# Two edits in the MLP of a hybrid encoder: a later row of norm factors, and a last step by plain products

## The chip, the cores and the metric

The kernel runs on one core of a Trainium2 chip, in one launch. The metric is the device time of that launch in microseconds; the median of three runs is 1983.71 us (1982.65 to 1984.13). The engines are named as in the profile: PE (TensorE's matrix products), PEld (its weight loads), DVE (VectorE), ACT (ScalarE), POOL (GpSimd), SP (SyncE, which here issues nearly all transfers).

## The reference, cut to what matters

x is 256 positions by 2048 channels, in float32. Two mixer layers, each followed by the MLP that this case is about:

```
def rmsnorm(x, g):
    y = xf * lax.rsqrt(jnp.mean(xf * xf, axis=-1, keepdims=True) + EPS)
    return y * g
def sq_relu_mlp(h, w_up, w_down):          # w_up 2048 x 8192, w_down 8192 x 2048
    a = jnp.square(jax.nn.relu(jnp.einsum('bsd,df->bsf', h, w_up)))
    return jnp.einsum('bsf,fd->bsd', a, w_down)
for i in range(2):
    ...
    x = x + sq_relu_mlp(rmsnorm(x, mlp_norm[i]), w_up[i], w_down[i])
return rmsnorm(x, final_norm)
```

## The kernel before, in words

**Products.** Every float32 operand is split into a high part (fp32r) and the rest. `split_piece` (L71) does so for 1024 columns of weights: ACT casts (`whi`, L73), DVE subtracts (`wlo`, L74); each side has four buffers. A block product is three matmuls into one PSUM bank (`mm3`, L105 to L108). `linear` (L110) computes one group of 512 output columns for both halves of the positions (t = 0, 1) in two banks of the pool `accp` (four banks), over 16 tiles of 128 inputs, and calls hooks before some of these tiles.

**Start of an MLP.** Before it, the last `linear` of the mixer's output projection ends, `add_x` adds its banks to x (L228, one add per t), `stats` squares x on ACT (L207), DVE and POOL turn the sums into the norm factor r per position (L213 to L218). r is needed along the free dimension, so L632 to L640 build a row of it: DVE scales the identity (`dg`, L634), PE multiplies ones by that (`rb`, L637, two float32 matmuls, which the trace shows as four), ACT copies the bank to `rb` (L639). r itself enters only later, in `hidden` (L687). The up products use x transposed and scaled by the norm's gain alone (`act`); the last quarter of it is made by `chunk(3)` (eight PE transposes, L197, then four copies on ACT, L187, and four on DVE, L188), a hook ahead of the fourth tile of the first up piece.

**Up.** One unit u makes 128 hidden channels for all positions: 16 weight tiles in two pieces (p = 0, 1), eight wide matmuls with the high weights (`high`, L659) and eight half as wide with the low ones (`low`, L651) for each. Units 0 and 1 open an MLP, their pieces interleaved: (unit 0, p 0), (unit 1, p 0), (unit 0, p 1), (unit 1, p 1). `hidden(q, z)` takes the two units of step q: times r, relu, square, split, and four block sums for the step below.

**Down.** Step q multiplies 256 hidden channels into 1024 of the 2048 output columns. As two by two blocks that is done by seven block products in place of eight: 21 matmuls, into the banks Q1, P2, Q3, Q5 (`accp`) and Q7, Q6, Q4 (the pool `tpp`, also four banks). Weights come by `s_load` (L709) and, summed, by `s_sums` (L720). Eight steps make a cycle, four cycles an MLP. In the code step c of cycle g issues unit 2q, the first three products of step q - 1, unit 2q + 1, and the other four; `more` is false in the very last step, which has no units left. After a cycle `s_end` (L738) adds the seven banks into x, and two `linear` calls do the other 1024 columns (n = 2, 3) for the cycle's 16 hidden tiles, with plain products. In the last cycle `stats` and `chunk` of the next norm follow: (0), (1) after `s_end`, (2) after n = 2, (3) after n = 3. In the second MLP `nxt` is `Final` (L576): its `stats` squares on ACT and multiplies by the gain on DVE (L589), its `chunk` does nothing, and n = 3 runs with three open banks and the kernel's end behind it.

**Order.** The text of the program is a list; a scheduler of the framework reorders it and fixes one order for each engine. On the chip every engine takes its list strictly in that order.

Of the kernel before, what the change touches and what calls it, by code (L numbers as in the profile page):

```python
# [12 lines left out]
F32 = mybir.dt.float32  # L13
# [6 lines left out]
P = 128  # L20
S = 256
# [7 lines left out]
PIECE = 2048  # L29
HALF = 1024  # L30
# [13 lines left out]
def trunk_kernel(ctx, tc, x_in, x_t, small, w_in_e0, w_in_e, w_out_e, w_in_o, w_lat2, w_uqn, w_uqr, w_ukv, w_out_o,  # L44
                 w_up0, w_up1, w_ds0, w_ds1, w_dn0, w_dn1, g_fin, dft_s, dft_c, rope, out):
    nc = tc.nc
# [9 lines left out]
    accp = ctx.enter_context(tc.tile_pool(name="accp", bufs=4, space=PSUM))  # L56
    tpp = ctx.enter_context(tc.tile_pool(name="tpp", bufs=4, space=PSUM))
# [5 lines left out]
    ones = const.tile([P, P], F32, name="ones")  # L63

    def load_raw(dram, n):
        raw = rawp.tile([P, PIECE], F32, tag="raw", name="raw")
        nc.sync.dma_start(out=raw[:, :n], in_=dram)
        return raw

    def split_piece(raw, o, n):  # L70
        hi = whp.tile([P, HALF], F32R, tag="whi", name="whi")  # L71
        lo = wlp.tile([P, HALF], F32R, tag="wlo", name="wlo")
        nc.scalar.copy(out=hi[:, :n], in_=raw[:, o:o + n])  # L73
        nc.vector.tensor_tensor(out=lo[:, :n], in0=raw[:, o:o + n], in1=hi[:, :n].bitcast(F32), op=ALU.subtract)  # L74
        return hi, lo
# [91 lines left out]
    def mm_kt(acc, t, a, part, j, n, first, last, c0=0, c1=None):  # L167
        sl = slice(t * P, (t + 1) * P)
        hi, lo = part
        c1 = c1 or n  # L170
        ws = slice(j * n + c0, j * n + c1)
        mm3(acc[t][:, c0:c1], a[0][:, sl], a[1][:, sl], hi[:, ws], lo[:, ws], first, last)
# [51 lines left out]
    def add_x(acc, n, scale=None, ts=(0, 1)):  # L224
        for t in ts:
            sl = xs[:, t, n * 512:(n + 1) * 512]
            if scale is None:
                nc.vector.tensor_tensor(out=sl, in0=acc[t], in1=sl, op=ALU.add)  # L228
            else:
                nc.vector.scalar_tensor_tensor(out=sl, in0=acc[t], scalar=scale[:, t:t + 1], in1=sl,  # L230
                                               op0=ALU.mult, op1=ALU.add)
# [388 lines left out]
    def mlp(ni, pend, w_up, w_ds, w_dn, nxt):  # L620
# [4 lines left out]
        G, C = 4, 8  # L625
# [6 lines left out]
        dg = stg.tile([P, 2, P], F32, tag="stg", name="dg", bufs=4)  # L632
        for t in range(2):
            nc.vector.tensor_scalar(out=dg[:, t, :], in0=ident, scalar1=ni.r[:, t:t + 1], scalar2=None, op0=ALU.mult)  # L634
        tp = tpp.tile([P, S], F32, tag="tp", name="rb")
        for t in range(2):
            nc.tensor.matmul(out=tp[:, t * P:(t + 1) * P], lhsT=ones, rhs=dg[:, t, :], start=True, stop=True)  # L637
        rb = mp_.tile([P, S], F32, name="rb")
        nc.scalar.copy(out=rb, in_=tp)  # L639
        rb2 = rb.rearrange("p (o c) -> p o c", o=1).broadcast_to([P, 2, S])  # L640

        def up_open(u):
            return u, tpp.tile([P, 512], F32, tag="tp", name="accT"), load_raw(w_up[u], PIECE)

        def up_piece(o, p, hooks):
            u, acc, raw = o
            hi, lo = split_piece(raw, p * HALF, HALF)

            def low():
                for k in range(8):  # L650
                    nc.tensor.matmul(out=acc[:, S:], lhsT=lo[:, k * P:(k + 1) * P], rhs=act[8 * p + k][0],  # L651
                                     start=False, stop=False)

            def high():
                for k in range(8):
                    kt = 8 * p + k
                    for f in hooks.get(kt, ()):
                        f()
                    nc.tensor.matmul(out=acc, lhsT=hi[:, k * P:(k + 1) * P], rhs=act[kt][2],  # L659
                                     start=kt == 0, stop=kt == 15)  # L660
            if p == 0:
                high()
                low()
            else:
                low()
                high()

        def up_end(o, z):
            u, acc, _ = o
            j = u % 2  # L670
            nc.scalar.copy(out=z[:, j, :], in_=acc[:, S:])  # L671
            nc.vector.tensor_tensor(out=z[:, j, :], in0=acc[:, :S], in1=z[:, j, :], op=ALU.add)  # L672

        def new_z():
            return stg.tile([P, 2, S], F32, tag="stg", name="z", bufs=4)
# [6 lines left out]
        def hidden(q, z):  # L682

            if q % 2 == 0:
                pool, tag = (mp_, "hx") if q // 2 % 5 == 4 else (a8p, "a8")
                slots[q // 2] = pool.tile([P, 2, 2, 512], F32R, tag=tag, name="hT")
            nc.vector.scalar_tensor_tensor(out=z, in0=z, scalar=0.0, in1=rb2, op0=ALU.max, op1=ALU.mult)  # L687
            h = stg.tile([P, 4, P], F32, tag="stg", name="h", bufs=4)
            nc.scalar.activation(out=h.rearrange("p a b -> p (a b)"), in_=z.rearrange("p a b -> p (a b)"),
                                 func=AF.Square)  # L690
            a = pair(q)
            split_from(h.rearrange("p a b -> p (a b)"), a[:, 0, :], a[:, 1, :])
            x = stg.tile([P, 4, P], F32, tag="stg", name="x", bufs=4)
            nc.vector.tensor_tensor(out=x[:, 0:2, :], in0=h[:, 0:2, :], in1=h[:, 2::-2, :], op=ALU.subtract)
            nc.vector.tensor_tensor(out=x[:, 2, :], in0=h[:, 1, :], in1=x[:, 0, :], op=ALU.subtract)
            nc.vector.tensor_tensor(out=x[:, 3, :], in0=h[:, 3, :], in1=x[:, 2, :], op=ALU.subtract)
            xh = mp_.tile([P, 4, P], F32R, tag="xh", name="xh")
            xl = mp_.tile([P, 4, P], F32R, tag="xl", name="xl")
            split_from(x, xh, xl)
            xs_of[q] = xh, xl  # L700
# [37 lines left out]
        def s_end(b):  # L738
# [11 lines left out]
            add(xc(0, 0), xc(0, 0), u)  # L750
            add(xc(0, 1), xc(0, 1), u, ALU.subtract)


        z = new_z()
        os = [up_open(u) for u in range(2)]
        for p in range(2):
            for j in range(2):
                up_piece(os[j], p, pend if j == p == 0 else {})
        for o in os:
            up_end(o, z)  # L760
        hidden(0, z)
        pend = {}
        for g in range(G):
            last = g == G - 1
            b = {}
            for c in range(1, C + 1):
                q = g * C + c
                f, l = c == 1, c == C
                more = q < G * C
                if more:  # L770
                    z = new_z()
                    o = up_open(2 * q)
                    for p in range(2):
                        up_piece(o, p, {})
                    up_end(o, z)
                r4, bh, bl = s_load(q - 1)
                if f:
                    b = {n: accp.tile([P, 512], F32, tag="acc", name=n) for n in ("Q1", "P2", "Q3", "Q5")}
                prod(b["Q1"], block(q - 1, 1), bh, bl, 0, f, l)
                prod(b["P2"], block(q - 1, 3), bh, bl, 2, f, l)  # L780
                prod(b["Q3"], xsum(q - 1, 3), bh, bl, 1, f, l)
                th, tl = s_sums(r4)
                if more:
                    o = up_open(2 * q + 1)
                    for p in range(2):
                        up_piece(o, p, {})
                    up_end(o, z)
                if f:
                    b.update({n: tpp.tile([P, 512], F32, tag="tp", name=n) for n in ("Q7", "Q6", "Q4")})
                prod(b["Q5"], xsum(q - 1, 0), th, tl, 1, f, l)  # L790
                prod(b["Q7"], xsum(q - 1, 1), th, tl, 0, f, l)
                if more:
                    hidden(q, z)
                prod(b["Q6"], xsum(q - 1, 2), th, tl, 2, f, l)
                prod(b["Q4"], block(q - 1, 2), th, tl, 3, f, l)
            s_end(b)
            if last:
                nxt.stats(0)
                nxt.stats(1)
                pend = {3: [lambda: nxt.chunk(0)], 7: [lambda: nxt.chunk(1)]}  # L800
            hT = [tuple(pair(g * C + k // 2)[:, i, (k % 2) * S:(k % 2 + 1) * S] for i in range(2)) for k in range(2 * C)]
            for n in (2, 3):
                if last and n == 3 and isinstance(nxt, Final):
                    linear(hT, list(range(16)), w_dn[2 * g + n - 2], 0, 512, halves=True, done=nxt.last, early=8)
                    st.close()
                    return {}
                acc = linear(hT, list(range(16)), w_dn[2 * g + n - 2], 0, 512, hooks=pend)
                pend = {}
                add_x(acc, n)
                if last:  # L810
                    nxt.stats(n)
                    pend = {3: [lambda n=n: nxt.chunk(n)]}
        st.close()
        return pend

# [405 lines left out]
```

## Time and profile before

| What | Value |
| --- | --- |
| median of the runs | 1983.71 us (1982.65 to 1984.13) |
| profiled execution, own time | 1980.53 us |
| its span, first to last instruction | 1978.7 us |
| PE busy, instructions | 1947.4 us (98%), 9868 |
| DVE, ACT busy | 1574.8 us (80%), 1133.6 us (57%) |
| mean granted TensorE clock | 0.997 |

A matmul's row shows from when to when it was in the array; the next one starts before it ends, so what a matmul costs is read from start to start. A bracket at a row's end is idle time of the engine just before, and what ended it. Busy time at a lower clock is busy time too: it takes the rows of granted clock to see it.

### The profile page before, as it was taken

The page shows a single profiled execution, that of the slowest core. Times are in us where ns is not written, and L with a number is a line of the kernel's source. Part 1 is how long each engine was busy: PE and PEld are TensorE (multiplying, and loading weights), DVE is VectorE, ACT ScalarE, POOL GpSimd, SP SyncE. Part 2 cuts the span into 40 slices and gives each one's busy share as a digit, 9 for nine tenths or more (in the row PEclk, how much of TensorE's full clock was granted, in tenths as well). Part 3 has the DMA queues.
Part 4 walks back from the last instruction along what each step waited for, and adds up shares of the span by engine and source line. Part 5 has one row for each costly group of instructions (what it writes and reads, how often), then busy time and mean ns, then how long its engine had stood idle before and what let it go on. Part 6 is the DMA issues. An engine that isn't in the chain of part 4 may idle for free.

```text
span 1978.7 us, 25204 instructions
## 1 busy us (share of the span) xinstructions
PE 1947.4 (98%) x9868; PEld 1650.1 (83%) x9868; DVE 1574.8 (80%) x2195; ACT 1133.6 (57%) x1583; POOL 11.6 (1%) x19
## 2 busy tenths in 40 slices
PE   8999999999999999999999999999999999999998
PEld 7887778888888888887888888788888888888877
DVE  7999768878896887887576667588968878896895
ACT  6787655645654664565554545456546645654654
POOL 0000000000000000000000000000000000000000
PEclk9999999999999999999999999999999999999999
DMA  8554545555555555454454546455555555555542
GB/s 296 200 174 167 210 155 175 204 199 189 192 192 213 192 195 206 174 198 148 160 189 149 190 169 241 165 192 191 181 209 190 204 198 189 192 191 213 192 170 107
DMA packets 55207, 374.00 MB, mean 189 GB/s; under 512 B 6064, under 2 KB 6448, under 8 KB 11824
## 3 DMA queue, kind: packets, MB, share of 16 engines
q1 hardware_dynamic: 54656, 370.69, 53.3%
q8 instruction: 77, 1.26, 0.3%
q0 software_dynamic: 144, 1.05, 0.1%
q10 hardware_dynamic: 288, 0.66, 0.1%
q14 instruction: 42, 0.34, 0.1%
HBM read 370.27 MB, written 2.10 MB: 188 GB/s over the span
## 4 chain that ended last, share of the span: by engine, by line
PE 93%; DVE 3%; DMA 1%; ACT 1%; issue 1%; POOL 0%; SPq 0%; POOLq 0%; DVEq 0%; ACTq 0%
PE accT L659 23%; PE acc L107 13%; PE acc L106 13%; PE acc L108 13%; PE accT L651 12%; PE Q L108 4%; PE Q L106 4%; PE Q L107 4%; PE tp L106 1%; PE tp L107 1%; PE tp L108 1%; DVE wlo L74 1%; PE P L107 1%; PE P L106 1%; PE P L108 1%
## 5 line engine op out<-in xcount | busy, mean ns | idle before, releaser
L74 DVE TENSOR_TENSOR wlo<-raw,whi 128x1024 fp32r<-128x1024 f32 (+2 forms) x568 | 683.4, 1211 | 312.5 <-ACT whi L73 311.9
L73 ACT CAST whi<-raw 128x1024 fp32r<-128x1024 f32 (+2 forms) x568 | 592.2, 1044 | 466.7 <-PE acc L108 307.9
L659 PE MATMUL accT<-n,whi 128*128 128x512 f32 x2048 | 514.5, 393 | 0.1
L659 PEld LDWEIGHTS accT<-n,whi 128*128 128x128 f32 x2048 | 377.3, 189 | 75.9 <-DVE z L672 0.6
L651 PEld LDWEIGHTS accT<-n,wlo 128*128 128x128 f32 x2048 | 262.9, 191 | 10.2
L651 PE MATMUL accT<-n,wlo 128*128 128x256 f32 x2048 | 266.0, 283 | 0.0
L107 PE MATMUL acc<-wlo,hT 128*128 128x512 f32 (+1 forms) x528 | 203.3, 385 | 0.1
L108 PE MATMUL acc<-whi,hT 128*128 128x512 f32 (+1 forms) x528 | 202.8, 384 | 0.0
L106 PE MATMUL acc<-whi,hT 128*128 128x512 f32 (+1 forms) x528 | 202.0, 384 | 0.0
L106 PE MATMUL acc<-whi,n 128*128 128x512 f32 (+2 forms) x480 | 181.1, 379 | 7.1 <-ACT whi L73 7.0
L107 PE MATMUL acc<-wlo,n 128*128 128x512 f32 (+2 forms) x480 | 178.4, 372 | 0.8 <-DVE wlo L74 0.8
L108 PE MATMUL acc<-whi,n 128*128 128x512 f32 (+2 forms) x480 | 178.7, 373 | 0.0
L722 DVE TENSOR_TENSOR sraw<-sraw 128x512 f32<-128x512 f32 x256 | 174.8, 683 | 1.0
L185 DVE TENSOR_TENSOR tl<-sraw,th 128x1024 fp32r<-128x1024 f32 x128 | 155.6, 1216 | 0.3
L184 ACT CAST th<-sraw 128x1024 fp32r<-128x1024 f32 x128 | 132.6, 1043 | 6.5 <-DVE sraw L722 3.5
L671 ACT COPY z<-accT 128x256 f32<-128x256 f32 x128 | 47.9, 375 | 150.7 <-PE accT L659 150.7
L185 DVE TENSOR_TENSOR bl<-sraw,bh 128x512 fp32r<-128x512 f32 (+1 forms) x128 | 118.5, 952 | 17.7 <-ACT bh L184 17.4
L184 ACT CAST bh<-sraw 128x512 fp32r<-128x512 f32 (+1 forms) x128 | 100.7, 834 | 30.5 <-DMA sraw<-in_w_ds 24.5
L107 PEld LDWEIGHTS acc<-wlo,hT 128*128 128x128 f32 x528 | 99.2, 188 | 22.0 <-DVE wlo L74 2.4
L106 PEld LDWEIGHTS acc<-whi,hT 128*128 128x128 f32 x528 | 99.2, 188 | 20.6 <-DVE xs L736 0.4
L108 PEld LDWEIGHTS acc<-whi,hT 128*128 128x128 f32 x528 | 99.2, 188 | 19.8
L106 PEld LDWEIGHTS acc<-whi,n 128*128 128x128 f32 x480 | 90.9, 190 | 21.2 <-ACT whi L73 7.8
(287 smaller groups left out, 2550.5 us busy)
## 6 DMA issues: line engine op xcount, KB each, us to landing
raw<-in_w_up SPq DMA_DIRECT2D x128, 1024.0 KB, 4.8
sraw<-in_w_ds SPq DMA_DIRECT2D x64, 1024.0 KB, 4.8
raw<-in_w_dn SPq DMA_DIRECT2D x64, 1024.0 KB, 4.9
raw<-in_w_in_o SPq DMA_DIRECT2D x28, 1024.0 KB, 4.9
raw<-in_w_in_e SPq DMA_DIRECT2D x20, 1024.0 KB, 5.0
raw<-in_w_out_e SPq DMA_DIRECT2D x16, 1024.0 KB, 5.0
raw<-in_w_out_o SPq DMA_DIRECT2D x16, 1024.0 KB, 4.8
raw<-in_w_in_e SPq DMA_DIRECT2D x6, 512.0 KB, 4.4
```

The costliest lines, as they stand in the source:

```text
L73: nc.scalar.copy(out=hi[:, :n], in_=raw[:, o:o + n])
L74: nc.vector.tensor_tensor(out=lo[:, :n], in0=raw[:, o:o + n], in1=hi[:, :n].bitcast(F32), op=ALU.subtract)
L106: nc.tensor.matmul(out=outs, lhsT=hi, rhs=rhi, start=first, stop=False)
L107: nc.tensor.matmul(out=outs, lhsT=hi, rhs=rlo, start=False, stop=False)
L108: nc.tensor.matmul(out=outs, lhsT=lo, rhs=rhi, start=False, stop=last)
L184: nc.scalar.copy(out=hi, in_=src)
L185: nc.vector.tensor_tensor(out=lo, in0=src, in1=hi.bitcast(F32), op=ALU.subtract)
L651: nc.tensor.matmul(out=acc[:, S:], lhsT=lo[:, k * P:(k + 1) * P], rhs=act[8 * p + k][0], start=False, stop=False)
L659: nc.tensor.matmul(out=acc, lhsT=hi[:, k * P:(k + 1) * P], rhs=act[kt][2], start=kt == 0, stop=kt == 15)
L671: nc.scalar.copy(out=z[:, j, :], in_=acc[:, S:])
L722: nc.vector.tensor_tensor(out=r4[:, o, :], in0=r4[:, i0, :], in1=r4[:, i1, :], op=ALU.add)
```

## The change

Two edits, both in `mlp`, which runs twice.

1. The two matmuls of the norm row and ACT's copy of it become a function, `rstd_row`, called after the p 0 pieces of units 0 and 1. The identity's scaling on DVE (`dg`) stays where it was.
2. In the last cycle the loop runs seven steps, not eight. The eighth step (hidden channels of step 31) is done by `rest`, after `linear` of n = 2: its weights come through the common weight buffers, unsummed, and its eight block products (24 matmuls) go into two pairs of `accp` banks, each pair added to x by `add_x`. So x's columns of n = 0, 1 are final only then: `stats` (0), (1), (2) come after `rest`, and their `chunk`s are hooks of n = 3. `more` goes, as every step left in the loop has units.

```
-        tp = tpp.tile([P, S], F32, tag="tp", name="rb")
-        for t in range(2):
-            nc.tensor.matmul(out=tp[:, t * P:(t + 1) * P], lhsT=ones, rhs=dg[:, t, :], start=True, stop=True)
         rb = mp_.tile([P, S], F32, name="rb")
-        nc.scalar.copy(out=rb, in_=tp)
...
+        def rstd_row():
+            tp = tpp.tile([P, S], F32, tag="tp", name="rb")
+            for t in range(2):
+                nc.tensor.matmul(out=tp[:, t * P:(t + 1) * P], lhsT=ones, rhs=dg[:, t, :], start=True, stop=True)
+            nc.scalar.copy(out=rb, in_=tp)
...
+        def rest(hT):
+            raw = load_raw(w_ds[G * C - 1], PIECE)
+            parts = [split_piece(raw, o, HALF) for o in (0, HALF)]
+            for n in range(2):
+                acc = [accp.tile([P, 512], F32, tag="acc", name=f"acc{t}") for t in range(2)]
+                for k in range(2):
+                    for t in range(2):
+                        mm_kt(acc, t, hT[2 * C - 2 + k], parts[k], 1 - n, 512, k == 0, k == 1)
+                add_x(acc, n)
...
                 up_piece(os[j], p, pend if j == p == 0 else {})
+            if p == 0:
+                rstd_row()
...
-            for c in range(1, C + 1):
+            steps = C - 1 if last else C
+            for c in range(1, steps + 1):
...
             s_end(b)
-            if last:
-                nxt.stats(0)
-                nxt.stats(1)
-                pend = {3: [lambda: nxt.chunk(0)], 7: [lambda: nxt.chunk(1)]}
...
-                if last:
-                    nxt.stats(n)
-                    pend = {3: [lambda n=n: nxt.chunk(n)]}
+                if last and n == 2:
+                    rest(hT)
+                    for m in (0, 1, 2):
+                        nxt.stats(m)
+                        pend[4 * m + 3] = [lambda m=m: nxt.chunk(m)]
+                elif last:
+                    nxt.stats(3)
+                    pend = {3: [lambda: nxt.chunk(3)]}
```

How the order on the engines moves, at three places. First PE at the start of the first MLP, before: acc1 is the last bank of the projection, accT_2299 and accT_2302 are units 0 and 1, n10 to n13 the transposed x in four parts, tp the banks of the transposes.

```order
L108 MATMUL acc1_2187<-whi_2258,ya1_1868 128x512
L637 MATMUL rb_2293<-dg_2290,ones_86 128x128 x2
L659 MATMUL accT_2299<-n10_1921,whi_2305 128x512 x3
L197 MATMUL tp_2312<-ident_84,xs_82 128x128 x4
L197 MATMUL tp_2321<-ident_84,xs_82 128x128 x4
L659 MATMUL accT_2299<-n10_1921,whi_2305 128x512
L659 MATMUL accT_2299<-n11_1922,whi_2305 128x512 x4
L651 MATMUL accT_2299<-n10_1921,wlo_2306 128x256 x4
L651 MATMUL accT_2299<-n11_1922,wlo_2306 128x256 x4
```

The same place on PE after the change, from the transposes on; the row ahead of them is the first three matmuls of unit 0 (accT_2295), and ahead of these stands the last of acc1.

```order
L197 MATMUL tp_2308<-ident_84,xs_82 128x128
L197 MATMUL tp_2317<-ident_84,xs_82 128x128
L661 MATMUL accT_2295<-n10_1921,whi_2301 128x512
L197 MATMUL tp_2308<-ident_84,xs_82 128x128 x3
L197 MATMUL tp_2317<-ident_84,xs_82 128x128 x3
L661 MATMUL accT_2295<-n11_1922,whi_2301 128x512 x4
L653 MATMUL accT_2295<-n10_1921,wlo_2302 128x256 x4
L653 MATMUL accT_2295<-n11_1922,wlo_2302 128x256 x4
L661 MATMUL accT_2298<-n10_1921,whi_2339 128x512 x4
L661 MATMUL accT_2298<-n11_1922,whi_2339 128x512 x4
L653 MATMUL accT_2298<-n10_1921,wlo_2340 128x256 x4
L653 MATMUL accT_2298<-n11_1922,wlo_2340 128x256 x4
L641 MATMUL rb_2359<-dg_2290,ones_86 128x128 x2
```

The row's matmuls moved behind 32 up matmuls and the eight transposes, and the first two transposes (one of each bank, both of t = 0) moved ahead of the fourth up matmul. Second, PE at the end of the first MLP's last cycle, before: the last product of the seventh step, the first rows of the eighth, and its end with the start of n = 2 (acc0).

```order
L108 MATMUL Q4_6892<-th_7703,hT_7616 128x512
L106 MATMUL Q1_6822<-bh_7781,hT_7616 128x512
L107 MATMUL Q1_6822<-bl_7782,hT_7616 128x512
...
L108 MATMUL Q6_6891<-th_7800,xl_7770 128x512
L107 MATMUL Q4_6892<-tl_7801,hT_7616 128x512
L108 MATMUL Q4_6892<-th_7800,hT_7616 128x512
L106 MATMUL acc0_7840<-whi_7844,hT_6454 128x512
```

After the change, same place:

```order
L108 MATMUL Q6_6891<-th_7703,xl_7627 128x512
L106 MATMUL Q4_6892<-th_7703,hT_7616 128x512
L107 MATMUL Q4_6892<-tl_7704,hT_7616 128x512
L108 MATMUL Q4_6892<-th_7703,hT_7616 128x512
L106 MATMUL acc0_7793<-whi_7797,hT_6454 128x512
L107 MATMUL acc0_7793<-wlo_7798,hT_6454 128x512
```

The 21 matmuls of the eighth step are gone from between the seventh step and n = 2; 24 stand behind n = 2. Third, ACT after the change, from the end of the first MLP's last cycle to its last chunk copies: casts of n = 2, `rest` and n = 3 (L73), squares of `stats` (L207), copies of `chunk` (L187; n_8017 to n_8019 are chunks 0 to 2).

```order
L73 CAST whi<-raw 128x1024 x7
L207 ACTIVATE junk,n2s<-xs 128x512 x2
L73 CAST whi<-raw 128x1024 x2
L207 ACTIVATE junk,n2s<-xs 128x512 x3
L73 CAST whi<-raw 128x1024
L207 ACTIVATE junk,n2s<-xs 128x512
L187 ACTIVATE n_8017<-tp,sm 128x256 x3
L73 CAST whi<-raw 128x1024
L187 ACTIVATE n_8017<-tp,sm 128x256
L73 CAST whi<-raw 128x1024
L187 ACTIVATE n_8018<-tp,sm 128x256 x4
L73 CAST whi<-raw 128x1024 x2
```

Six squares and twelve chunk copies now stand between the casts of n = 3. Before, four squares and eight copies stood between those of n = 2, and two squares and four copies between those of n = 3.

## Rows read from the trace of the kernel before

**Rows 1.** The page: span, and busy time of each engine.
```profile
span 1978.7 us, 25204 instructions
...
PE 1947.4 (98%) x9868; PEld 1650.1 (83%) x9868; DVE 1574.8 (80%) x2195; ACT 1133.6 (57%) x1583; POOL 11.6 (1%) x19
```

**Rows 2.** Waits of PE: who waited for whom, total us, times, longest.
```profile
PE rb L637 <- DVE dg L634: 8.2, 2, 4.1
...
PE Q L106 <- ACT hT L184: 3.7, 2, 1.9
```

**Rows 3.** Timeline of PE, first MLP's start: start us, length us, instruction, idle before.
```profile
253.17 0.39 PE L108 MATMUL acc<-whi,ya 128*128 128x512 f32 x1
257.65 1.19 PE L637 MATMUL rb<-dg,ones 128*128 128x128 f32 x4 [4.09 <-DVE dg L634]
...
263.27 1.11 PE L651 MATMUL accT<-n,wlo 128*128 128x256 f32 x8
264.22 2.00 PE L659 MATMUL accT<-n,whi 128*128 128x512 f32 x8
266.06 2.08 PE L651 MATMUL accT<-n,wlo 128*128 128x256 f32 x16
```

**Rows 4.** Timeline of PE, second MLP's start.
```profile
1270.69 0.39 PE L108 MATMUL acc<-whi,yc 128*128 128x512 f32 x1
1275.21 0.68 PE L637 MATMUL rb<-dg,ones 128*128 128x128 f32 x4 [4.13 <-DVE dg L634]
1275.65 0.96 PE L659 MATMUL accT<-n,whi 128*128 128x512 f32 x3
...
1282.86 2.08 PE L651 MATMUL accT<-n,wlo 128*128 128x256 f32 x16
```

**Rows 5.** Windows: length, busy PE, PEld, DVE, ACT, POOL; clock, DMA share, GB/s.
```profile
256.00:257.00 1.00, 0.00 (x0) 0.00 (x0) 0.33 (x2) 0.01 (x1) 0.51 (x1) 0.50 0.98 418
...
1277.00:1278.00 1.00, 1.00 (x8) 1.00 (x6) 0.00 (x0) 0.47 (x1) 0.00 (x0) 0.50 0.55 221
...
906.00:908.00 2.00, 0.79 (x4) 0.30 (x3) 2.00 (x3) 1.41 (x3) 0.00 (x0) 1.00 0.90 381
```

**Rows 6.** Timeline of DVE and ACT, first MLP's start.
```profile
253.10 1.28 DVE L228 TENSOR_TENSOR xs<-acc,xs 128x512 f32<-128x512 f32 x2
...
254.54 0.63 ACT L207 ACTIVATE junk<-xs 128x512 bf16<-128x512 f32 x1
...
257.21 0.48 DVE L634 TENSOR_SCALAR dg<-ident,n1r 128x128 f32<-128x128 f32 x2 [0.80 <-POOL n1r L218]
...
261.01 0.47 ACT L187 ACTIVATE n<-tp,sm 128x256 fp32r<-128x256 f32 x1 [1.76 <-PE tp L197]
...
261.52 0.48 DVE L188 SCALAR_TENSOR_TENSOR n<-tp,sm,n 128x256 fp32r<-128x256 f32 x1 [3.82 <-ACT n L187]
```

**Rows 7.** Timeline of PE, last cycles of the first and second MLP.
```profile
902.35 0.40 PE L108 MATMUL Q<-th,hT 128*128 128x512 f32 x1
...
911.31 0.39 PE L106 MATMUL acc<-whi,hT 128*128 128x512 f32 x1
...
1917.35 0.40 PE L108 MATMUL Q<-th,hT 128*128 128x512 f32 x1
...
1926.33 0.39 PE L106 MATMUL acc<-whi,hT 128*128 128x512 f32 x1
```

**Rows 8.** Timeline of PE: n = 2 after the third cycle; chunk(0) in the last.
```profile
746.57 0.39 PE L106 MATMUL acc<-whi,hT 128*128 128x512 f32 x1
...
915.88 1.03 PE L197 MATMUL tp<-ident,xs 128*128 128x128 f32 x8
916.67 0.48 PE L108 MATMUL acc<-whi,hT 128*128 128x512 f32 x1
```

**Rows 9.** The page's groups: busy us, mean ns | idle before, what ended most.
```profile
L74 DVE TENSOR_TENSOR wlo<-raw,whi 128x1024 fp32r<-128x1024 f32 (+2 forms) x568 | 683.4, 1211 | 312.5 <-ACT whi L73 311.9
L73 ACT CAST whi<-raw 128x1024 fp32r<-128x1024 f32 (+2 forms) x568 | 592.2, 1044 | 466.7 <-PE acc L108 307.9
```

More of the change, by code (lines that the diff above doesn't have):

```diff
@@ L765, in mlp @@
             b = {}
-            for c in range(1, C + 1):
+            steps = C - 1 if last else C
+            for c in range(1, steps + 1):
                 q = g * C + c
[L768 to L775, printed above, removed]
+                f, l = c == 1, c == steps
+                z = new_z()
+                o = up_open(2 * q)
+                for p in range(2):
+                    up_piece(o, p, {})
+                up_end(o, z)
                 r4, bh, bl = s_load(q - 1)
@@ L782, in mlp @@
                 th, tl = s_sums(r4)
[L783 to L787, printed above, removed]
+                o = up_open(2 * q + 1)
+                for p in range(2):
+                    up_piece(o, p, {})
+                up_end(o, z)
                 if f:
@@ L791, in mlp @@
                 prod(b["Q7"], xsum(q - 1, 1), th, tl, 0, f, l)
-                if more:
-                    hidden(q, z)
+                hidden(q, z)
                 prod(b["Q6"], xsum(q - 1, 2), th, tl, 2, f, l)
@@ L807, in mlp @@
                 acc = linear(hT, list(range(16)), w_dn[2 * g + n - 2], 0, 512, hooks=pend)
-                pend = {}
                 add_x(acc, n)
-                if last:
-                    nxt.stats(n)
-                    pend = {3: [lambda n=n: nxt.chunk(n)]}
+                if last and n == 2:
[6 more added lines that the diff above has]
+                    pend = {3: [lambda: nxt.chunk(3)]}
         st.close()
```

## The prediction

> **What bounds the kernel now.** I read the page first: PE is busy 1947.4 of 1978.7 us [rows 1], so all that PE is free to lose is 31.3 us, and a change is worth what it takes from PE's own line: idle time, a lower clock, or matmuls. Second, PE's waits: the norm row (`rb`) waits for `dg` twice, 8.2 us in all, and the first product of the last cycles' eighth step waits for `hidden`'s cast twice, 3.7 us [rows 2]. The reader is to see that both sit exactly where the two edits are. Third, PE's timeline at these four places [rows 3, 4, 7], read from start to start: the busy share hides that the stretch behind an idle time can be slow. Fourth, the granted clock: at the starts of both MLPs it is 0.50 of full speed, the 1.2 GHz level, a while after PE stopped, with products running at that level in the second; it is 1.00, 2.4 GHz, within the eighth step though PE was idle for half of that window [rows 5].
>
> Rates at full clock: a wide up matmul (266.06 - 264.22) / 8 = 0.23; eight lows 264.22 - 263.27 = 0.95 [rows 3]; the row's four matmuls 1275.65 - 1275.21 = 0.44 [rows 4]; eight transposes 916.67 - 915.88 = 0.79 [rows 8]. I take 0.23 for every wide matmul.
>
> **Edit 1, the start of an MLP.** Nothing is removed or added; two matmuls and a copy move behind 32 up matmuls and eight transposes. Before, the projection's last matmul starts at 253.17, so PE is free for the next at 253.40. The row of 16 lows at 266.06 is (unit 1, p 0) and then (unit 0, p 1); its second half starts at 266.06 + 0.95 = 267.01 [rows 3]. By then PE has done all that in the new order stands ahead of the same point: 3 wide (0.69), eight transposes (0.79), 5 wide (1.15), eight lows (0.95), eight wide (1.84), eight lows (0.95), 6.37 in all, and the row (0.44): 6.81. Without a wait the new order gets there at 253.40 + 6.81 = 260.21: 6.80 us earlier. In the second MLP PE is free at 1270.92, so 1277.73 against 1282.86 + 0.95 = 1283.81: 6.08 earlier [rows 4]. Sum 12.88. Of it 8.2 is the wait [rows 2], and the rest, 4.7, is nearly all the half clock behind it.
>
> Does a wait take its place? The first two transposes need only the add of t = 0, and PE reaches them at 253.40 + 0.69 = 254.09; the other six need both adds, which end at 253.10 + 1.28 = 254.38 [rows 6], and PE reaches them after two transposes and a matmul, at 254.09 + 0.20 + 0.23 = 254.52. That is even; I take no wait, and 0.3 a layer as the other end. The up matmuls' weights are no issue, since ACT is ahead of PE: most of the idle time before its casts is waiting for PE to free a buffer [rows 9]. The row now stands 6.37 behind 253.40, at 259.77. `dg` started at 257.21 [rows 6]; now one chunk copy (0.47) stands between the squares on ACT, and two of DVE's chunk instructions (0.48 each) ahead of it on DVE, so it is done by 257.21 + 0.47 + 0.96 + 0.48 = 259.12 at the latest. The row is the fifth tile on `tpp`'s four banks and needs the first transposes' bank back, but the DVE instruction that frees it stands ahead of `dg`. No wait, margin 0.65; the other end is 2 a layer, half of what it waited before [rows 2]. What reads the row (`hidden`, L687) needs both units done, over 5 us later on PE.
>
> Does the clock stay up? With no gap left the case is that of any other hand-over. The row nearest to it is the eighth step: PE busy 0.79 of 2.00 us and the clock still 1.00 [rows 5]. So I take full clock, and half clock as the other end: before, PE took 266.06 - 257.65 = 8.41 and 1282.86 - 1275.21 = 7.65 from the row to the group of 16, where full rates give 6.81 - 0.95 = 5.86; the lower clock cost at most 2.55 + 1.79 = 4.3. The Trainium skill (TensorE: Matmul & The Clock Gate, part 4 on PE-mode transpose) says that transposes do not count as busy time for the clock in the way matmuls do. By that rule eight transposes right at the hand-over would be time in which the clock can fall, and the sum would be smaller by what a fall costs. This trace has chunk(0)'s transposes amid matmuls at full rate [rows 8], which is no sign of it.
>
> **Edit 2, the last cycle.** Before, from the slot behind the seventh step to the first matmul of n = 2: 911.31 - 902.35 - 0.23 = 8.73 us, and 1926.33 - 1917.35 - 0.23 = 8.75 in the second MLP [rows 7]. All of that leaves this place: 21 matmuls are 4.83, the rest is waiting for `hidden` of step 31, which nothing covers as there are no units left. What comes back, behind n = 2, is 24 matmuls, 24 x 0.23 = 5.52. Gain 3.21 + 3.23 = 6.44. `hidden` (31) is now needed by n = 2's fifteenth hidden tile, 14 x 6 x 0.23 = 19 us later, so its chain is covered.
>
> What is late next? n = 2 takes two banks that `s_end` must free. The third cycle ends with the same list, units ahead and all, and there n = 2 starts with no idle time before it [rows 8]: no wait; other end, all of edit 2's gain. The step's four sums and their splits leave DVE and ACT; two casts, two subtracts and four adds come. The transfers are as many as before, one of them in the common queue of weight buffers behind n = 2's: 24 matmuls per transfer as in `linear`. Then n = 3: six squares (0.63 each) and, in the first MLP, twelve copies on ACT (0.47) and twelve on DVE (0.48) [rows 6] stand between its casts. ACT then has 8 x 1.04 [rows 9] + 3.8 + 5.6 = 17.7 of n = 3's 96 x 0.23 + 3 x 0.79 = 24.5 us; DVE 8 x 1.21 + 5.8 and the adds. The third cast is the first behind squares: these need `rest`'s first adds, so 12 x 0.23 + 1.28 + 1.26 = 5.3 us after `rest` begins, its end 6.3; PE needs it at 5.52 + 2 x 2.76 = 11.0. Covered. In the second MLP n = 3 opens three banks, the third of which needs `rest`'s last pair's first add (0.64) soon after: 0 to 1 us, I take 0. Below nothing there is no room: PE has no other idle time in these places.
>
> **Sum.** 12.88 + 6.44 = 19.3 us less. Against the profiled execution's own time of 1980.53 that is 1961.2; the runs shown are 3.2 above it in the median, so 1983.7 - 19.3 = 1964.4.
>
> **The rivals.**
> - *The clock falls all the same* at both starts. For it: it fell there before, in one case after PE had stood still only from 253.56 to 256 [rows 3, 5]. Against: no such gap is left. 4.3 less: 1968.7. By the rule on transposes of the Trainium skill (TensorE: Matmul & The Clock Gate, part 4) it would go this way.
> - *The row waits at its new place.* For it: the margin of 0.65, and casts that wait for PE stand on ACT between the chunk copies. 2 a layer: 1968.4.
> - *The end gives nothing*: `s_end` or `rest` hands over late by as much as was saved. For it: four banks, all taken by Q1, P2, Q3, Q5 at the hand-over. Against: the third cycle [rows 8]. 1964.4 + 6.4 = 1970.8.
> - *Slower: n = 3 of the last cycle is bound by ACT and DVE.* The moved work lies between n = 3's casts, on strict lists; if PE drains its four buffers and then stands for all of it: first MLP 3.8 + 5.6 + 5.8, second 3.8 of squares + 6 x 0.64 of gains, and `rest`'s adds 2 x 2.56: 15.2 + 7.6 + 5.1 = 27.9, so 1992.3. It makes the kernel slower by more than can be told from 23.3 us uncovered on, most of it. Against: the 4.7 us to spare at the third cast.
>
> That the change doesn't do what it says is not one: the order shows the rows moved.
>
> **How the numbers follow.** Forecast 0.78; clock 0.06; row 0.05; end 0.06; slower rival 0.05, of which I give 0.03 to a partial form that ends within 0.2% (4 us, about what a measurement of this kernel can tell from no change) and 0.02 to the full one. The first four are all faster by over 0.2%: 0.95, 0.03, 0.02. The range reaches up to the end case, 1971; down to 1960.5, since all unknown costs but the runs' own offset to the profiled execution (their lowest is 2.1, their highest 3.6 above it) were already taken at their lower end.
>
> **What would show it.** After: PE's waits have no `rb` row and no `Q` rows for hT and xh; the clock is 1.00 through both starts; the row's matmuls start some 6.4 us after the projection's last slot; n = 2 of the last cycle starts 0.23 behind the seventh step's last product; 24 matmuls stand between n = 2 and n = 3 with no bracket behind. I am wrong if a new PE wait on a cast (L73) or on x (L228) shows in n = 3, if `rb` still has a wait, or if the clock rows at the starts still show 0.50.

## The result and the profile after

The changed kernel takes 1961.62 us in the median (1960.07 to 1964.19), the kernel before beside it 1983.92: ratio 0.9888, 95% interval 0.9875 to 0.9900, so 22.2 us less (19.8 to 24.8). Forecast were 19.3 us less and 1964.4. On another chip, beside the two halves of the change, it was 0.9891 (0.9877 to 0.9906). The profiled execution took 1960.07 us, against 1980.53 before: 20.5 less.

The page of the kernel after, as [rows 1]:

```profile
span 1958.3 us, 25215 instructions
...
PE 1942.3 (99%) x9874; PEld 1648.3 (84%) x9874; DVE 1572.0 (80%) x2191; ACT 1130.2 (58%) x1579; POOL 11.7 (1%) x19
```

PE's idle time fell from 31.3 to 16.0 us. That is 15.3 of the 20.4 us by which the span fell; the other 5.1 were busy time, in the main matmuls at half clock (the filled wait below puts these at 4.0). PE's waits after, all of them (who waited for whom, total us, times, longest), against [rows 2]:

```profile
PE acc L106 <- ACT whi L73: 6.1, 2, 5.7
PE acc L107 <- DVE wlo L74: 0.8, 1, 0.8
PE ssum L398 <- DVE sq L395: 0.3, 1, 0.3
PE tp L355 <- DVE glu L375: 0.3, 1, 0.3
PE accT L661 <- DVE z L674: 0.2, 1, 0.2
```

Neither `rb` nor a product (`Q`) is among them. Both waits of the longest row left, for a cast (L73), lie in the kernel's own start, at 5.70 and 12.29 us; none lies in n = 2 or n = 3 of a last cycle. PE's timeline at the first MLP's start, as [rows 3], then at the second's, as [rows 4] (start us, length us, instruction):

```profile
252.54 0.39 PE L108 MATMUL acc<-whi,ya 128*128 128x512 f32 x1
252.77 0.84 PE L661 MATMUL accT<-n,whi 128*128 128x512 f32 x3
253.45 0.38 PE L197 MATMUL tp<-ident,xs 128*128 128x128 f32 x2
...
255.50 1.11 PE L653 MATMUL accT<-n,wlo 128*128 128x256 f32 x8
256.44 2.00 PE L661 MATMUL accT<-n,whi 128*128 128x512 f32 x8
258.29 1.11 PE L653 MATMUL accT<-n,wlo 128*128 128x256 f32 x8
259.24 0.60 PE L641 MATMUL rb<-dg,ones 128*128 128x128 f32 x4
259.60 1.20 PE L653 MATMUL accT<-n,wlo 128*128 128x256 f32 x8
...
1258.54 0.39 PE L108 MATMUL acc<-whi,yc 128*128 128x512 f32 x1
...
1265.24 0.60 PE L641 MATMUL rb<-dg,ones 128*128 128x128 f32 x4
1265.60 1.20 PE L653 MATMUL accT<-n,wlo 128*128 128x256 f32 x8
```

No bracket stands at the end of any of these rows: PE goes from the projection into the up products, and the row waits for nobody. The projection's last matmul to (unit 0, p 1) is 259.60 - 252.54 = 7.06 us in both MLPs. Why the row doesn't wait is DVE's line for `dg`:

```profile
256.81 0.48 DVE L634 TENSOR_SCALAR dg<-ident,n1r 128x128 f32<-128x128 f32 x2 [0.32 <-POOL n1r L218]
```

It is done at 257.29, 1.95 us before the row starts. The windows (length, busy PE, PEld, DVE, ACT, POOL, granted clock, DMA share, GB/s) that answer to the 0.50 in [rows 5]:

```profile
253.00:255.00 2.00, 2.00 (x14) 1.75 (x13) 1.71 (x3) 2.00 (x5) 0.00 (x0) 1.00 0.69 164
...
257.00:259.00 2.00, 2.00 (x14) 1.75 (x12) 2.00 (x5) 1.17 (x3) 0.00 (x0) 1.00 0.92 373
...
1263.00:1265.00 2.00, 2.00 (x14) 1.75 (x13) 2.00 (x5) 1.17 (x3) 0.00 (x0) 1.00 0.94 377
```

The clock stays at full speed, 2.4 GHz. Last, PE at the end of the last cycle's products in both MLPs, as [rows 7]:

```profile
893.56 0.39 PE L108 MATMUL Q<-th,hT 128*128 128x512 f32 x1
893.79 0.39 PE L106 MATMUL acc<-whi,hT 128*128 128x512 f32 x1
...
1900.19 0.39 PE L108 MATMUL Q<-th,hT 128*128 128x512 f32 x1
1900.42 0.39 PE L106 MATMUL acc<-whi,hT 128*128 128x512 f32 x1
```

n = 2 starts 0.23 us behind the seventh step's last product, one slot, where before there were 8.96 and 8.98.

### The profile page after: what moved, and what is told of

Same layout as the page of the kernel before. It is cut to its first block, busy times and chain, and to the rows that moved or that the text cites. A ratio compares the mean times of both kernels' runs of the same rounds, so it can differ in the third digit from the quotient of the medians.

```text
span 1958.3 us, 25215 instructions
## 1 busy us (share of the span) xinstructions
PE 1942.3 (99%) x9874; PEld 1648.3 (84%) x9874; DVE 1572.0 (80%) x2191; ACT 1130.2 (58%) x1579; POOL 11.7 (1%) x19
## 5 line engine op out<-in xcount | busy, mean ns | idle before, releaser
L74 DVE TENSOR_TENSOR wlo<-raw,whi 128x1024 fp32r<-128x1024 f32 (+1 forms) x572 | 688.7, 1212 | 298.9 <-ACT whi L73 298.3
L73 ACT CAST whi<-raw 128x1024 fp32r<-128x1024 f32 (+1 forms) x572 | 596.5, 1044 | 455.4 <-PE acc L108 297.9
L107 PE MATMUL acc<-wlo,hT 128*128 128x512 f32 (+1 forms) x544 | 209.6, 385 | 0.1
L108 PE MATMUL acc<-whi,hT 128*128 128x512 f32 (+1 forms) x544 | 209.0, 384 | 0.0
L106 PE MATMUL acc<-whi,hT 128*128 128x512 f32 (+1 forms) x544 | 208.4, 385 | 0.1
L724 DVE TENSOR_TENSOR sraw<-sraw 128x512 f32<-128x512 f32 x248 | 170.0, 686 | 1.0
L185 DVE TENSOR_TENSOR tl<-sraw,th 128x1024 fp32r<-128x1024 f32 x124 | 151.3, 1220 | 0.2
L184 ACT CAST th<-sraw 128x1024 fp32r<-128x1024 f32 x124 | 128.4, 1043 | 5.3 <-issue 2.9
L185 DVE TENSOR_TENSOR bl<-sraw,bh 128x512 fp32r<-128x512 f32 x124 | 115.3, 954 | 17.9 <-ACT bh L184 17.5
L106 PEld LDWEIGHTS acc<-whi,hT 128*128 128x128 f32 x544 | 102.2, 188 | 21.7 <-DVE xs L738 1.0
L108 PEld LDWEIGHTS acc<-whi,hT 128*128 128x128 f32 x544 | 102.2, 188 | 20.4
L184 ACT CAST bh<-sraw 128x512 fp32r<-128x512 f32 x124 | 97.5, 834 | 31.5 <-DMA sraw<-in_w_ds 25.5
```

The costliest lines, as they stand in the source:

```text
L106: nc.tensor.matmul(out=outs, lhsT=hi, rhs=rhi, start=first, stop=False)
L107: nc.tensor.matmul(out=outs, lhsT=hi, rhs=rlo, start=False, stop=False)
L108: nc.tensor.matmul(out=outs, lhsT=lo, rhs=rhi, start=False, stop=last)
L184: nc.scalar.copy(out=hi, in_=src)
L185: nc.vector.tensor_tensor(out=lo, in0=src, in1=hi.bitcast(F32), op=ALU.subtract)
L724: nc.vector.tensor_tensor(out=r4[:, o, :], in0=r4[:, i0, :], in1=r4[:, i1, :], op=ALU.add)
```

## The experiments

One table, read from PE's timelines, for all profiled executions but two, which change what stands at the end and have their own numbers below ("rest ahead" and "seven products behind"). "Start" runs from the projection's last matmul to the first product of the MLP's first step. "End" is the time from the slot behind the seventh step's last product to n = 2 in the last cycle; in the new form its work, 24 matmuls, stands behind n = 2 and is not in it.

| kernel | start, MLP 1 | start, MLP 2 | end, MLP 1 | end, MLP 2 |
|---|---|---|---|---|
| before | 25.00 | 24.29 | 8.73 | 8.75 |
| before again, 1 | 24.90 | 24.27 | 8.74 | 11.05 |
| before again, 2 | 24.95 | 24.27 | 8.76 | 10.90 |
| before again, 3 | 25.28 | 24.99 | 8.95 | 10.97 |
| row only | 18.30 | 18.27 | 8.92 | 11.04 |
| end only | 24.97 | 25.20 | 0.00 | 0.00 |
| after | 18.29 | 18.29 | 0.00 | 0.00 |
| after again | 18.29 | 18.27 | 0.01 | 0.00 |
| wait filled with matmuls | 22.65 | 22.68 | 8.93 | 10.94 |
| wait filled with transposes | 22.68 | 22.68 | 10.89 | 8.72 |
| row behind one piece | 18.97 | 18.99 | 0.01 | 0.00 |
| end filled with matmuls | 23.99 | 25.11 | 8.75 | 8.73 |

**The two halves, and both again.** The first is the kernel before with the row moved alone:

```diff
                 up_piece(os[j], p, pend if j == p == 0 else {})
+            if p == 0:
+                rstd_row()
```

> The kernel before with edit 1 alone: the row's products behind the first up products, the last cycle as it was. My theory: PE loses its idle time and its half clock at both MLP starts and nothing else, so 6.8 us at the first and 6.0 at the second, 12.8 us less than before; PE's waits still have the Q rows for hT and xh (3.7 us), no rb row. Rival (a part of the gain is not local: the rest of the kernel also runs better by 2 to 3 us once PE is ahead at the start): 15 us less or more.

Measured: ratio 0.9936 (0.9924 to 0.9948) to the kernel before on the same chip, 12.7 us less (10.3 to 15.1), median 12.8. PE's waits keep the products' row and have none for `rb`:

```profile
PE Q L106 <- ACT hT L184: 3.8, 2, 1.9
```

The second is the kernel before with the last step by plain products alone:

```diff
-            for c in range(1, C + 1):
+            steps = C - 1 if last else C
+            for c in range(1, steps + 1):
...
+                if last and n == 2:
+                    rest(hT)
```

> The kernel before with edit 2 alone: the last of the eight steps done by plain products behind n = 2, the row as it was. My theory: 3.2 us less in each MLP, 6.5 in all; the two starts still have the wait for dg (8.2 us) and a granted clock of 0.50 behind it. Rival (the end's gain rests on edit 1 having put the whole stream ahead): 3 us or less. The sum of this run's gain and that of the row alone should be that of both edits; if the two make 19.3 and both edits 22, something is left that neither has.

Measured: 0.9964 (0.9952 to 0.9976), 7.1 us less (4.8 to 9.5), median 7.2; the row's wait is there as in [rows 2]:

```profile
PE rb L637 <- DVE dg L634: 8.2, 2, 4.1
```

And the kernel after, unchanged:

> The kernel after once more, beside the two halves on one chip. My theory (its parts add up, and about 1.6 us of the first profile's gain, in the second and third step of the first MLP, was a late transfer of that one execution of the kernel before): 19 to 20 us less than the kernel before. Rival (the excess over 19.3 is a steady effect of the change): 22 us less again.

Measured: 20.1 us less by the medians, 21.6 by the ratio (18.6 to 24.4). The halves add up, 12.8 + 7.2 = 20.0, so neither needs the other. Whether the whole is 19 to 20 or 22 these intervals can't say; the table says more, below.

**Idle time or clock.** PE gets something to do while it waits for `dg`; the row comes no earlier. What is added is dummy work, whose result nobody reads.

```diff
             nc.vector.tensor_scalar(out=dg[:, t, :], in0=ident, scalar1=ni.r[:, t:t + 1], scalar2=None, op0=ALU.mult)
+        fill = accp.tile([P, 512], F32, tag="acc", name="fill")
+        for _ in range(17):
+            nc.tensor.matmul(out=fill, lhsT=act[0][0][:, :P], rhs=act[0][2], start=True, stop=True)
```

> The kernel before with 17 wide matmuls added ahead of the row's own, into a bank that nobody reads, so that PE works (17 x 0.23 = 3.9 us) while it waits for dg; the row itself comes no earlier. My theory (4.7 of the 12.8 us are the half clock that follows the idle time): granted clock 1.00 through both starts, PE takes 5.9 us from the row to the group of 16 in place of 8.4 and 7.7, and the kernel is 4 to 4.7 us faster than before although it does more. Rival (the stretch behind the row is slow for another reason, late operands or banks): the clock may stay up, but the 8.4 and 7.7 us stay and the kernel takes the same time as before.

Measured: 0.9969 (0.9958 to 0.9980), 6.1 us less (4.0 to 8.3), 4.7 by the medians, though it does 34 matmuls more. PE's timeline at the first start, and a window of it:

```profile
253.33 0.39 PE L108 MATMUL acc<-whi,ya 128*128 128x512 f32 x1
253.56 4.01 PE L637 MATMUL fill<-n 128*128 128x512 f32 x17
257.82 0.68 PE L640 MATMUL rb<-dg,ones 128*128 128x128 f32 x4 [0.25 <-DVE dg L634]
...
263.86 2.08 PE L654 MATMUL accT<-n,wlo 128*128 128x256 f32 x16
```

```profile
257.00:259.00 2.00, 1.75 (x10) 1.22 (x9) 0.48 (x2) 0.37 (x1) 0.35 (x1) 1.00 0.97 352
```

From the row to the group of 16 it now takes 263.86 - 257.82 = 6.04 us where [rows 3] have 8.41, with the clock at 1.00. The rival, late operands or banks, would have kept the 8.41: it falls. In the table the clock alone is worth 25.00 - 22.65 = 2.35 and 24.29 - 22.68 = 1.61. With transposes for filling:

```diff
+        for i in range(40):
+            nc.tensor.transpose(out=fill[:, i % 4 * P:(i % 4 + 1) * P], in_=xs[:, 0, i % 4 * P:(i % 4 + 1) * P], identity=ident)
```

> As the filled wait, but the filling is 40 transposes of 128x128 (40 x 0.1 = 4.0 us) in place of the wide matmuls. If transposes keep the clock up as matmuls do: clock 1.00 through both starts, 4 to 4.7 us faster than before. If they count as idle time for the clock: 0.50 behind the row as before, and the time of before within 0.5 us.

Measured: 0.9966 (0.9953 to 0.9979), 6.7 us less (4.2 to 9.3). The timeline and a window that holds transposes alone:

```profile
255.25 4.53 PE L637 MATMUL fill<-ident,xs 128*128 128x128 f32 x40
259.61 0.61 PE L640 MATMUL rb<-dg,ones 128*128 128x128 f32 x4
...
265.57 2.08 PE L654 MATMUL accT<-n,wlo 128*128 128x256 f32 x16
```

```profile
257.00:259.00 2.00, 2.00 (x21) 2.00 (x20) 1.08 (x3) 0.84 (x4) 0.65 (x1) 1.00 1.01 426
```

259.61 - 255.25 = 4.36 us of nothing but transposes, clock 1.00, and 5.96 from the row to the group of 16. So transposes keep the clock as matmuls do here. The Trainium skill (TensorE: Matmul & The Clock Gate, part 4 on PE-mode transpose) says otherwise; for these f32 transposes the measurement decides. The trace calls them MATMUL, so whether they run in the mode that the page speaks of is not shown.

**How much cover the row needs.** The row one piece earlier:

```diff
-            if p == 0:
-                rstd_row()
+                if j == p == 0:
+                    rstd_row()
```

> The kernel after, but the row's products stand behind the first piece alone, some 2.8 us earlier than in the kernel after. dg was done at 257.29 there and PE would be at the row at about 256.4, so PE waits 0.9 us at each start. My theory (a wait this short costs only itself): rb waits of 0.8 to 0.9 us, twice, granted clock 1.00, 1.6 to 1.8 us slower than after. Rival (any stop there takes the clock down): 0.50 behind it, 5 us and more slower than after.

Measured: 0.9906 (0.9889 to 0.9922), in the median 0.7 us above the kernel after again and 2.5 above its first timing, which were on other chips and tell little; the table tells more, 0.68 + 0.70 = 1.4 us over the kernel after. Timeline and window:

```profile
259.20 0.68 PE L641 MATMUL rb<-dg,ones 128*128 128x128 f32 x4 [0.43 <-DVE dg L634]
```

```profile
257.00:259.00 2.00, 1.78 (x13) 1.48 (x11) 1.65 (x7) 2.00 (x5) 0.69 (x1) 1.00 1.06 426
```

The wait is 0.43, half of what was expected, in part since the scheduler put two low products of the next piece ahead of the row. Besides, the row starts at 259.20, before the second of `dg`'s two instructions is done at 259.25, so its first matmul needs only the first. A stop this short costs little beside itself, and the clock stays up at both starts.

**Place or form, at the end.** The new form in the old place, ahead of n = 2:

```diff
+            if last:
+                rest(hT)
             for n in (2, 3):
...
-                    rest(hT)
```

> The kernel after, but the plain products of the last step stand ahead of n = 2, where the seven products stood, so in the old place in the new form. My theory (the place is what counts): PE waits for the cast of hidden of step 31 again, 1.9 us and more in each MLP, with half a dozen smaller brackets; 4 to 6 us slower than after. Rival (the form counts: the four sums with their splits made the gap): no more than 1 us slower than after.

Measured: 0.9948 (0.9927 to 0.9968), 10.1 us slower than the kernel after again in the median: the direction of my theory, about twice its size, and no half dozen of smaller brackets. PE in the first MLP's last cycle, and a window:

```profile
895.77 0.40 PE L108 MATMUL Q<-th,hT 128*128 128x512 f32 x1
896.84 0.50 PE L106 MATMUL acc<-whi,hT 128*128 128x512 f32 x1 [0.68 <-ACT hT L184]
...
902.29 0.39 PE L108 MATMUL acc<-whi,hT 128*128 128x512 f32 x1
904.60 0.50 PE L106 MATMUL acc<-whi,hT 128*128 128x512 f32 x1 [1.92 <-DVE xs L228]
...
905.45 0.63 PE L106 MATMUL acc<-whi,hT 128*128 128x512 f32 x1
...
908.82 0.40 PE L108 MATMUL acc<-whi,hT 128*128 128x512 f32 x1
```

```profile
906.00:908.00 2.00, 2.00 (x6) 1.52 (x5) 2.00 (x3) 1.50 (x5) 0.00 (x0) 0.50 0.00 0
```

From the seventh step's last product to the MLP's end it takes 56.84 us, the kernel after 51.98; in the second MLP 54.88 against 49.96. Of the 4.9 in the first MLP, start to start, the wait for `hidden`'s cast is 0.84; a second wait, for `rest`'s own adds into x (L228), is 2.08; eight matmuls at half clock lose 908.82 - 905.45 - 8 x 0.23 = 1.5; the other 0.4 is mostly single matmuls that start some 0.1 late. I had expected the first, too long, and neither of the others. The place is what counts: the seven products there take 55.34 us over the same stretch in the first profile of the kernel before, so the plain form is no better there.

The old form in the new place: `rest` does the seven products, with sums and output adds of its own, 21 matmuls in place of 24.

```diff
-            raw = load_raw(w_ds[G * C - 1], PIECE)
...
+            r4, bh, bl = s_load(q)
+            b = {n: accp.tile([P, 512], F32, tag="acc", name=n) for n in ("Q1", "P2", "Q3", "Q5")}
+            prod(b["Q1"], block(q, 1), bh, bl, 0, True, True)
...
+            s_end(b)
```

> The kernel after, but the eighth step behind n = 2 is done by the seven products (21 matmuls, with their own sums and a second set of output adds) in place of 24 plain ones. If only the place counts and PE's matmuls are the price: 3 x 0.23 = 0.7 us less per MLP, 1.4 less than after, with no waits of PE at n = 3. Rival (the form counts: the step's sums on ACT and DVE and its output adds come between n = 3's casts and the banks come free later): PE waits in n = 3, 1 to 6 us more than after.

Measured: 0.9882 (0.9869 to 0.9894), in the median 2.6 us less than the kernel after again and 0.9 less than its first timing, with no wait of PE in n = 3. The interval overlaps that of the kernel after; the timelines agree better: 51.47 and 49.46 us from the seventh step's last product to the MLP's end, 0.51 and 0.50 less. So it is a version that is 1.0 us faster by its PE line, less than the 1.4 expected; where the 0.2 per MLP went I did not find.

**The clock in the old end.** The table shows what the first profile did not: the old end takes 8.7 to 8.95 us at 8 of 14 places and 10.9 to 11.05 at 6. At the second MLP of the kernel before it is 8.75 only in the profile that I predicted from. The same kernel again, unchanged, as a test of that:

> The kernel before, unchanged. Ratio to itself 1 within its interval, which tells what a difference is worth here. At its two eighth steps: by the theory that the clock falls there in some executions of the kernel before too, 0 to 2 places with 0.50 and a stretch of 10 to 11.3 us in place of 8.7; by the rival (only the edited kernels had it) both 8.7 at 1.00, as in the first profile.

> The kernel before once more, for its profile: over this and the run beside it, about two of four eighth steps with the clock at 0.50 by the theory, none by the rival.

> The kernel before a third time, for its profile: with the two runs beside it, about three of six eighth steps with the clock at 0.50 by the theory, none by the rival.

Measured: ratio to itself 1.0000 (0.9991 to 1.0009); 11.05, 10.90 and 10.97 in the second MLP, three of six places. The first repeat, PE's timeline and two windows, the one in the first MLP's end, the other in the second's:

```profile
1918.54 0.40 PE L108 MATMUL Q<-th,hT 128*128 128x512 f32 x1
1920.92 0.50 PE L106 MATMUL Q<-bh,hT 128*128 128x512 f32 x1 [1.98 <-ACT hT L184]
...
1924.27 0.80 PE L106 MATMUL Q<-bh,xh 128*128 128x512 f32 x1 [0.67 <-ACT xh L184]
...
1925.29 0.63 PE L106 MATMUL Q<-th,xh 128*128 128x512 f32 x1
1925.71 0.63 PE L107 MATMUL Q<-tl,xh 128*128 128x512 f32 x1
...
1929.82 0.40 PE L106 MATMUL acc<-whi,hT 128*128 128x512 f32 x1
```

```profile
907.00:909.00 2.00, 0.79 (x4) 0.30 (x3) 2.00 (x3) 1.44 (x3) 0.00 (x0) 1.00 0.94 389
...
1924.00:1926.00 2.00, 1.73 (x4) 1.46 (x5) 1.90 (x3) 0.21 (x1) 0.00 (x0) 0.50 0.29 123
```

The matmuls start 0.42 apart in place of 0.23. The first bracket, 1.98, is that of [rows 2], 1.9 at the longest; the loss is behind it, in no wait. At a fourth of the six places, the third repeat's first MLP, the clock fell too, though its end took only 8.95:

```profile
909.18 0.53 PE L106 MATMUL Q<-bh,xh 128*128 128x512 f32 x1 [0.34 <-ACT xh L184]
```

```profile
906.00:908.00 2.00, 2.00 (x6) 1.54 (x5) 2.00 (x4) 1.05 (x1) 0.00 (x0) 0.50 0.86 238
```

Here the slow matmuls lie between the two waits, so that the second wait, 1.2 in the first profile, shrinks to 0.34 and hides most of the loss. With the row alone the first MLP's end (8.92) is the same case, at 0.50 from 898 to 901. So the clock fell at 8 of the 14 places, and 6 of them show it in their length.

And the waits of the old end filled, as at the start (15 dummy matmuls):

```diff
+                if not more:
+                    fill = tpp.tile([P, 512], F32, tag="tp", name="fill")
+                    for _ in range(9):
+                        nc.tensor.matmul(out=fill, lhsT=act[0][0][:, :P], rhs=act[0][2], start=True, stop=True)
                 prod(b["Q1"], block(q - 1, 1), bh, bl, 0, f, l)
                 prod(b["P2"], block(q - 1, 3), bh, bl, 2, f, l)
+                if not more:
+                    for _ in range(6):
+                        nc.tensor.matmul(out=fill, lhsT=act[0][0][:, :P], rhs=act[0][2], start=True, stop=True)
```

> The kernel before with 15 wide matmuls added, into a bank that nobody reads, where PE waits in the eighth step of both last cycles (9 ahead of the first product, 6 ahead of the xh products: 15 x 0.23 = 3.4 us, as long as the two waits of 2.04 and 1.39). Theory formed after the first eight runs (in the old form the clock falls behind these waits in some executions, as it did at 4 of 8 such places, and costs 1 to 3 us where it falls): granted clock 1.00 through both eighth steps, 8.7 to 9.3 us from the slot behind the seventh step to n = 2 in both, and 1 to 3 us faster than before on the mean. Rival (the matmuls at half rate were waiting for something else): the stretch stays at 11 us in some of them, no gain.

Measured: 0.9990 (0.9981 to 0.9999), 2.0 us less (0.2 to 3.8), with 30 matmuls more; 8.75 and 8.73 at the ends, clock 1.00 in both:

```profile
905.00:907.00 2.00, 2.00 (x10) 1.43 (x8) 2.00 (x4) 1.49 (x3) 0.00 (x0) 1.00 0.83 344
```

```profile
1922.00:1924.00 2.00, 1.95 (x9) 1.27 (x8) 2.00 (x4) 1.20 (x2) 0.00 (x0) 1.00 0.91 381
```

So the 11 us are half clock, and three of the four profiles of the kernel before paid about 2.2 us for it, once each.

## Why the prediction was right, and which term was too small

- **Edit 1, 6.80 + 6.08.** Measured by the same reading, 13.84 - 7.06 = 6.78 and 13.12 - 7.06 = 6.06; with the row alone 12.7 us of time. Right to 0.1, and so is its division into wait and clock: the filled wait gives 3.96 for the clock where 4.3 was the most.
- **No wait in its place.** Right, and with more room than I gave it: margin 1.95, not 0.65. I had put a chunk copy and two of DVE's chunk instructions ahead of `dg` and added up their lengths, 1.43. They do stand there, DVE's two at 255.19 and 256.01, but `dg` waits for POOL in any case (its bracket, 0.32): it starts 256.81 - 252.54 = 4.27 behind the projection's last matmul, where it was 257.21 - 253.17 = 4.04.
- **The clock stays up.** Right in all five profiled executions of the new start, and in that with the row behind one piece. But the row that I argued from, the eighth step with PE busy 0.79 of 2.00 us at clock 1.00 [rows 5], was no proof: the same waits took the clock down at four of the eight such places in the four profiles of the kernel before. What held is the first half of the argument, that no gap is left. The rival by the rule on transposes falls by the filled transposes.
- **Edit 2, 3.21 + 3.23.** For the profile that it was read from, the term is right: from the seventh step's last product to the MLP's last matmul it took 55.34 and 53.28 us before and takes 51.98 and 49.96 after, 3.36 and 3.32 less. For the kernel before as it mostly runs it is the term that was too small: "911.31 - 902.35 - 0.23 = 8.73 us, and ... 8.75 in the second MLP". In the four profiles of the kernel before the eight places have a mean of 9.61, with 8.7 as the least, so what leaves is 0.87 more per MLP, 1.7 in all; over all 14 places of the old end, 9.74, it is 2.0. With that the sum is 21.0 to 21.3, against 22.2 (19.8 to 24.8) and 21.6 (18.6 to 24.4). What came back was right: nothing waits in n = 2 or n = 3.
- **The base.** The profile stood at 1980.53, 3.2 below the median, and I took that as an offset of no meaning. The three others took 1984.06, 1982.95 and 1984.75; each has at the second end the 2.2 to 2.3 us that it lacked. So the greater part of the offset was the missing part of the term. The mean granted clock is on record for 62 more executions of this kernel: 0.991 to 0.996, where that profile has 0.997. The forecast was read from the mildest case on record, and that was chance.
- **What neither edit explains.** The two first profiles differ by 1.1 us more than 19.3. Stretches that no edit touches account for it: up to the first MLP 0.6, the second and third step of the first MLP 1.6 (there DVE got a weight late in the kernel before), the second MLP's steps -1.0. The late weight is in the first repeat of the kernel before and not in the other two, so it comes and goes with no edit.
- **The slower rival**, n = 3 bound by ACT and DVE, is refuted: no wait on a cast or on x there.

## What to carry to other kernels

A wait in the matmul stream is priced by start-to-start times of the same work with and without it, since what follows at half clock stands in no wait; where the wait can't go, dummy matmuls in it tell how much is clock, and may pay by themselves. A clock that stayed up behind a wait in one profile is no proof: read such a stretch in three or four profiles before its length goes into a sum. Work that hangs on the last result of a chain goes behind work that doesn't, even at the price of more matmuls (24 for 21 here; the 21 behind n = 2 were 1.0 us better still).

## What the chip did that I had not expected

The same instructions, with the same waits at the same place (2.04 and 1.39 us, start to start, with seven matmuls between), kept the clock at 1.00 at 6 of 14 places and fell to 0.50 at 8, 2.2 us longer at 6 of these and 0.2 at 2. The four profiles of the unchanged kernel alone have 4 and 4. The Trainium skill (TensorE: Matmul & The Clock Gate, part 1) says that the number of matmuls that one kernel runs at the low clock at its start varies from run to run; the trace agrees, with 18 to 25 such matmuls at the start of the four profiles of the kernel before (0.21 us apart, later ones of the size 0.12), and here it is so in mid-kernel too. The idle times of 4.3 us at the old starts took the clock down at all 12 places (no start under 23.99 us, where the filled waits give 22.65); those of 0.6 us in the kernel with the row behind one piece at neither; those of 0.84 and 2.08 us with `rest` ahead of n = 2 at both. And 40 transposes in a row kept it up, as told above.
